# A state-space layer whose late adaLN loads get six buffers instead of three ahead, with x parked in DRAM meanwhile, and a weight cast issued ahead of a Silu

## The chip, the cores and the metric

The kernel runs on one core of one Trainium2 chip. The core has one matrix engine (TensorE, written PE; its weight loads are written PEld), a vector engine (VectorE, DVE), a scalar engine (ScalarE, ACT), a general engine (GpSimd, POOL) and a synchronisation engine (SyncE, SP) that here mainly issues DMA transfers. The metric is the device time of one execution in microseconds (us); the figure for a kernel is the median over its runs.

## The reference, cut to what matters

The model is a trunk of two layers on 512 tokens of width 1024 in float32. Layer 0 mixes tokens by a gated short convolution, layer 1 by a Mamba-2 state-space layer (SSD) with 8 groups of 4 heads; each is followed by a SwiGLU FFN. Every one of the four sub-layers normalises its input, applies a shift, a scale and a gate that come from the conditioning vector c (adaLN), and adds its result to x:

```
mod = (silu(c) @ ada_w + ada_b).reshape(bsz, DEPTH, 2, 3, D_MODEL)
...
z, xbc, dt_raw = split(h @ w_in, [M_D_INNER, M_D_INNER + M_CONV_DIM])
xbc = silu(causal_depthwise_conv(xbc, conv_w) + conv_b)
...
y = ssd_chunked(xs, dt, a, bm, cm) + d_skip * xs
y = rms_normalize((y * silu(z)).reshape(..., g, M_D_INNER // g)) * norm_g
return y @ w_out
...
gate, up = split(h @ w_in, 2);  return (silu(gate) * up) @ w_out
```

`ada_w` is 1024 x 12288, so the product `silu(c) @ ada_w` reads 48 MB for a single row of output. It is not bound to any place in the program: each block of 1024 columns only has to be done before the sub-layer that uses it.

## The kernel before, in words

**Arithmetic.** Matrix products run on PE in a split form: each float32 weight tile is split into a high part (a cast on ACT, `split_w` L212, L230, or `Units.split` L616) and a low part (a subtraction on DVE, L213, L231, L617), and three matmuls (L285 to L287) take the place of one. A weight tile can be used when ACT and then DVE have passed over it.

**The FFNs.** Part of each FFN's first product is computed in "units" (class `Units`; 12 units in the first FFN, 16 in the second) by a scheme of seven products P1 to P7, of 12 matmuls of 128x128x256 each, in place of eight. Three weight sets are split for each unit: X, Y and Z (and a half one, S). The products accumulate in three banks sA, sB, sC; between them small steps (`c11`, `c12`, `c22`, `c21`) move finished quarters to the output and apply the Silu (for a gate, in even units) or the product with the gate (in odd units). For PE, the order in the loop is P1 of unit u, P7 of u-1, P5 of u, P2 of u, P4 of u-1, P6 of u, P3 of u. `c12(v)`, with v = u-1, ends in a Silu on ACT (L677) where v is even, `split_x(u + 1)` casts X of the next unit (ACT L616) and subtracts (DVE L617), and `c22(v)` (DVE L681) drains bank sA, which P4 of u-1 then takes. The same order is written out again in the second FFN.

**The state-space layer.** The eight groups run one behind the other in a pipeline written out by hand, with a loop over g = 1 to 6 for the middle ones. For each group PE makes the projections of x, B, C and z (`project`, `project_z`), the states (`states`, matmuls `st` L1773), the terms from earlier chunks (`yo` L1812) and within a chunk (`yd` L1823), and sums for the norm (`sums`, `ssg` L1855). DVE makes the convolution (`cu` L1677), the inputs of the states (`step_a`: `xw` L1744, `xdt` L1746), the decay factors (`csb` L1800), the running state (`prev` L1778, L1780), the outputs (`y` L1828, `yg`) and the low halves of the weights (L231). Small tables of cumulated sums (cs, ecs) go to DRAM (`cs_d` L1654, `ecs_d` L1656) and are read back broadcast over partitions.

**The late adaLN work.** Four blocks of 1024 columns of `ada_w` are treated here (`late_sums`). Each is eight loads of 512 KB (`ada_st`, 32 in all), each followed by one DVE instruction (`ada_madd` L123 to L127) that multiplies by a value of silu(c) and adds to `ada_acc`; after eight of them `ada_fold` (L140) and one PE matmul (`ada_fin` L147) finish the block. The buffers of the loads come from the pool `ysp` (five buffers, which `ada_acc` and the norm's squares share); load n+3 is requested right behind the sum that uses load n. A call `late(5)` at the head of each round of the loop gives five steps, and `late(1)` ahead of `step_a` one more while g < 5.

**The residual x** lies in four tiles of 128 x 1024 float32 (`xt`, tags x0 to x3 of pool `hp`). The state-space layer uses it at its start, to normalise it, and at its end, to add to it.

**What sets the order.** PE, ACT and DVE run in the order in which the code issues their work (`manual_schedule`). The queue on SP, which issues nearly all loads in this layer, is ordered by the scheduler, and works strictly in that order: a DMA that waits for a buffer holds up those behind it.

Of the kernel before, what the change touches and what calls it, by code (L numbers as in the profile page):

```python
# [8 lines left out]
F32 = mybir.dt.float32  # L9
# [7 lines left out]
P = 128  # L17
T = 512
D = 1024
KD = D // P  # L20
# [11 lines left out]
MUL, ADD, SUB = ALU.mult, ALU.add, ALU.subtract  # L32
# [6 lines left out]
def trunk_kernel(  # L39
# [7 lines left out]
    dma = nc.sync.dma_start  # L47
# [534 lines left out]
    class Units:  # L582
# [34 lines left out]
            dve.tensor_tensor(dst[:, 1], src, dst[:, 0].bitcast(F32), SUB)  # L617

        def split_x(self, u):
            self.split("X", u, whole(), self.staged[u][0][:, 0:8, :])  # L620

        def split_y(self, u):
            self.split("Y", u, whole(), self.staged[u][1].rearrange("p s k f -> p (s k) f"))
# [117 lines left out]
    def whole():  # L741
        return whl_p.tile([P, 2, 8, P], F32R, tag="whl", name="whl")
# [9 lines left out]
    with ExitStack() as ph:  # L752
# [582 lines left out]
        with tc.manual_schedule(engines={PE_ENGINE, mybir.EngineType.SP, mybir.EngineType.Activation,  # L1335
# [51 lines left out]
            for u in range(UN1):  # L1387
                v = u - 1
                end = u == UN1 - 1
                if not end:  # L1390
                    un.fetch(u + 2)
                else:
                    more_n = load_w([(f_w_in[0], (fu + 1) * P, P), (f_w_in[0], DFF + fu * P, P)], later=splits)
                un.product(u, "P1")
                if u:
                    un.c12(v)
                else:
                    up(3, acc[1])
                un.split_x(u + 1)
                if u:  # L1400
                    un.product(v, "P7")
                un.keep(u, "A", 0, lo_)
                un.product(u, "P5")
                if u:
                    un.c22(v)
                low_parts(1)
                un.product(u, "P2")
                un.keep(u, "C", 1, hi_)
                if u:
                    un.product(v, "P4")  # L1410
# [12 lines left out]
                if end:  # L1423
                    for op in splits[2]:
                        op()
                    more_n += load_w([(f_w_in[0], DFF + (fu + 1) * P, P)], later=splits)
                else:
                    un.split_y(u + 1)
                un.product(u, "P3")
                un.keep(u, "A", 0, hi_)  # L1430
                if not end:
                    un.split_s(u + 1)
            u = UN1 - 1
# [151 lines left out]
    with ExitStack() as ph:  # L1585
# [4 lines left out]

        cs_d = dram.tile([NH, T], F32, name="cs_d")
        ecs_d = dram.tile([NH, T], F32, name="ecs_d")

        dt_tok = consts.tile([P, NH, NCH], F32, name="dt_tok")
        cs_tok = consts.tile([P, NH, NCH], F32, name="cs_tok")
# [3 lines left out]
        def flat(ap):  # L1599
            return ap.rearrange("p a b -> p (a b)")  # L1600
# [270 lines left out]
        def late_sums():  # L1871

            uh = tmp.tile([P, 256], F32, tag="uh", name="four", bufs=2)
            sets, st = (64, 72, 80, 88), []

            def load(n):
                if n < KD * len(sets):
                    q0, k = sets[n // KD], n % KD
                    st.append(flat(ysp.tile([P, 2, T], F32, tag="ys", name="ada_st")))
                    dma(st[n], ada_w[k * P:(k + 1) * P, q0 * P:q0 * P + D])  # L1880

            acc = flat(ysp.tile([P, 2, T], F32, tag="ys", name="ada_acc"))
            for n in range(3):
                load(n)
            yield uh[:, 0:P]
            for i, q0 in enumerate(sets):
                for k in range(KD):
                    ada_madd(acc, st[i * KD + k], k)
                    load(i * KD + k + 3)
                    yield  # L1890
                part = uh[:, P + 32 * (i % 2):P + 32 * (i % 2) + 32]
                ada_fold(acc, part)
                fins_late.append(late_end(q0, part))
                yield
# [8 lines left out]
        def late(n):  # L1903
            for _ in range(n):
                next(steps_late, None)
# [30 lines left out]
        with tc.manual_schedule(engines={PE_ENGINE, mybir.EngineType.Activation, mybir.EngineType.DVE}):  # L1936
            cur, nxt, nn = Group(0), Group(1), Group(2)
            nxt.weights(0)
            convs = [cur.conv(i, lead_ps[1 + i]) for i in range(4)]
            rest(0)  # L1940
            raw = dt_raw(lead_ps[0])
# [79 lines left out]
            for g in range(1, NG - 1):  # L2021
# [3 lines left out]
                conv2 = [nxt.project(i) for i in range(2)]  # L2025
                prev.root()
                late_fin()
                late(5)
                nxt.later[3][0]()
                prev.norm()  # L2030
                next(conv2[0])
# [4 lines left out]
                nxt.later[4][0]()  # L2036
                next(conv2[1])
                cur.e_sub(1)
                if g < 5:
                    late(1)  # L2040
                cur.step_a()
                for q in range(2):
                    cur.e_exp(q)
# [34 lines left out]
                cur.sums()  # L2078

            assert next(steps_late, 0) == 0  # L2080
            prev, cur = cur, nxt
            next(parts[0])
            prev.root()
# [53 lines left out]
    with ExitStack() as ph:  # L2137
# [137 lines left out]
        with tc.manual_schedule(engines={PE_ENGINE, mybir.EngineType.SP, mybir.EngineType.Activation,  # L2275
# [60 lines left out]
            for u in range(UN):  # L2336
# [4 lines left out]
                elif last:  # L2341
                    tail = []
                    n12 = load_w([(w1, 21 * P, P), (w1, DFF + 20 * P, P)], later=tail)
                product(u, "P1")
                if u:
                    c12(v)
                else:
                    t_four(1)
                    up(3, acc2)
                split_x(u + 1)  # L2350
                if u:
                    product(v, "P7")
                keep(u, "A", 0, LO)
# [210 lines left out]
```

## Time and profile before

| | |
|---|---|
| Median of 3 runs | 1333.65 us (1332.31 to 1334.56) |
| The profiled execution | 1333.14 us, its span 1331.4 us |
| Mean granted PE clock | 0.997 |
| PE busy | 1310.1 us of the span |
| DVE busy | 1022.0 us |
| ACT busy | 723.0 us |
| POOL busy | 109.8 us |
| First FFN, the units | 253 to 374.5 us from the span's start |
| State-space groups 0 to 6 (between their `ssg` matmuls) | 597.1 to 890.4 us |
| Second FFN, the units | 1035.7 to 1194.1 us |

The profile is of one execution. A row of a group of instructions gives the busy time, the mean length of one in ns, and the idle time ahead of it on its engine with what ended it. A row of waits reads: engine, the tile it was to work on and its line, what it waited for, then total us, number of times, longest. A row of windows gives, for a stretch of time, its length and each engine's busy time with the number of instructions, then the granted PE clock, the mean busy share of the 16 DMA engines and GB/s. A row of the timeline gives the start, the length, the instruction and, in brackets, the idle time ahead of it.

### The profile page before, as it was taken

Reading aid. Unit: us, or ns where it says so; the run is one execution under the profiler, and the core shown is the slowest. Engines: PE = TensorE matmul, PEld = TensorE weight load, DVE = VectorE, ACT = ScalarE, POOL = GpSimd, SP = SyncE. Lnnn points to the kernel's source line nnn. Section 1 sums busy time; section 2 is a strip of 40 time slices with the busy share of each in tenths; the row PEclk is TensorE's granted clock in tenths of the full one; section 3 lists DMA queues with packets and bytes.
Section 4 is the critical chain, followed back from the end, with each engine's and each line's share of the span. In section 5 each row is a group of like instructions: output and inputs, shape, how many; then the busy total and the mean of one; then the engine's idle time right before and its main releaser. Section 6 shows DMA issues by size and latency. Waiting matters only on the chain.

```text
span 1331.4 us, 20439 instructions
## 1 busy us (share of the span) xinstructions
PE 1310.1 (98%) x7869; PEld 1148.7 (86%) x7869; DVE 1022.0 (77%) x1533; ACT 723.0 (54%) x1258; POOL 109.8 (8%) x135
## 2 busy tenths in 40 slices
PE   8999999999999999999999999999999999999998
PEld 7788889999988888898788878888789999998886
DVE  5577767888866887758788978887587777776888
ACT  5333246455432566646765567655574455554665
POOL 0000000111100330000000000000000111101330
PEclk9999999999999999999999999999999999999999
DMA  9767651699878875136654456423251788869871
GB/s 309 231 221 240 222 173 41 175 258 253 206 224 280 204 135 150 45 95 211 206 191 152 140 198 206 127 96 112 95 154 38 197 208 215 210 173 289 183 133 63
DMA packets 224276, 234.85 MB, mean 176 GB/s; under 512 B 10148, under 2 KB 176948, under 8 KB 223156
## 3 DMA queue, kind: packets, MB, share of 16 engines
q1 hardware_dynamic: 203856, 191.03, 46.2%
q0 software_dynamic: 16176, 29.63, 12.8%
q10 hardware_dynamic: 4148, 12.90, 2.9%
q8 instruction: 61, 1.00, 0.3%
q14 instruction: 35, 0.29, 0.1%
HBM read 201.66 MB, written 2.24 MB: 153 GB/s over the span
## 4 chain that ended last, share of the span: by engine, by line
PE 75%; DVE 10%; DMA 9%; ACT 4%; issue 2%; SPq 0%; ACTq 0%; DVEq 0%; POOLq 0%
PE sA L654 10%; PE y L387 8%; PE ip L285 7%; PE ip L287 7%; PE ip L286 7%; PE sC L654 5%; PE cA L2272 4%; DMA ada_st<-in_ada_w_dram 4%; PE cA L1310 3%; PE sB L654 2%; PE li L936 2%; PE li L285 2%; PE li L287 2%; PE li L286 2%; DVE cu L1677 2%; DMA wsu<-wsu 2%
## 5 line engine op out<-in xcount | busy, mean ns | idle before, releaser
L285 PE MATMUL ip<-h,whl 128*128 128x512 f32 x648 | 256.3, 396 | 0.2 <-DVE cv L1036 0.2
L287 PE MATMUL ip<-h,whl 128*128 128x512 f32 x648 | 252.5, 390 | 0.0
L286 PE MATMUL ip<-h,whl 128*128 128x512 f32 x648 | 252.4, 390 | 0.0
L285 PEld LDWEIGHTS ip<-h,whl 128*128 128x128 f32 x648 | 121.9, 188 | 26.5 <-issue 1.8
L287 PEld LDWEIGHTS ip<-h,whl 128*128 128x128 f32 x648 | 121.7, 188 | 25.8
L286 PEld LDWEIGHTS ip<-h,whl 128*128 128x128 f32 x648 | 121.9, 188 | 24.4
L654 PE MATMUL sA<-tq,whl 128*128 128x256 f32 x1008 | 131.3, 284 | 1.7 <-DVE g L681 1.6
L654 PEld LDWEIGHTS sA<-tq,whl 128*128 128x128 f32 x1008 | 125.3, 192 | 3.6 <-DVE g L681 2.9
L127 DVE SCALAR_TENSOR_TENSOR ada_acc<-ada_st,csil,ada_acc 128x1024 f32<-128x1024 f32 x70 | 89.7, 1281 | 28.3 <-DMA ada_st<-in_ada_w_dram 27.4
L231 DVE TENSOR_TENSOR whl<-wst,whl 128x1024 fp32r<-128x1024 f32 x70 | 85.2, 1221 | 25.8 <-ACT whl L230 25.8
L617 DVE TENSOR_TENSOR whl<-wsu,whl 128x1024 fp32r<-128x1024 f32 x58 | 70.9, 1223 | 33.2 <-ACT whl L616 33.2
L387 PE MATMUL y<-whlo,ys 128*128 128x512 f32 x384 | 89.4, 392 | 0.0
L387 PEld LDWEIGHTS y<-whlo,ys 128*128 128x128 f32 x384 | 71.7, 188 | 16.0 <-issue 0.7
L285 PE MATMUL li<-h,whl 128*128 128x256 f32 x288 | 83.2, 289 | 0.0
L287 PE MATMUL li<-h,whl 128*128 128x256 f32 x288 | 81.5, 283 | 0.0
L286 PE MATMUL li<-h,whl 128*128 128x256 f32 x288 | 81.5, 283 | 0.0
L230 ACT CAST whl<-wst 128x1024 fp32r<-128x1024 f32 x70 | 72.8, 1041 | 3.1 <-DMA wst<-in_f_w_in_dram 2.1
L616 ACT CAST whl<-wsu 128x1024 fp32r<-128x1024 f32 x58 | 60.7, 1046 | 14.5 <-PE sB L654 12.2
L1229 POOL DMA_DIRECT2D sg<-sg x28 | 24.4, 871 | 529.5 <-DMA sg<-in_f_w_in_dram 353.0
L1677 DVE SCALAR_TENSOR_TENSOR cu<-ip,cols,cu 128x511 f32<-128x511 f32 (+2 forms) x84 | 62.8, 747 | 3.5 <-ACT cu L1674 1.4
L2272 PE MATMUL cA<-whlo,ao 128*128 128x512 f32 x264 | 61.0, 390 | 0.4 <-DVE c L2477 0.2
L2272 PEld LDWEIGHTS cA<-whlo,ao 128*128 128x128 f32 x264 | 49.3, 188 | 11.5 <-ACT whlo L2237 1.2
(381 smaller groups left out, 2659.5 us busy)
## 6 DMA issues: line engine op xcount, KB each, us to landing
ada_st<-in_ada_w_dram SPq DMA_DIRECT2D x96, 512.0 KB, 6.6
wsu<-in_f_w_in_dram SPq DMA_DIRECT2D x30, 512.0 KB, 5.8
sg<-in_f_w_in_dram SPq DMA_DIRECT2D x56, 256.0 KB, 3.5
wsu<-in_f_w_in_dram SPq DMA_DIRECT2D x56, 256.0 KB, 4.7
wst<-in_m_w_in_dram SPq DMA_DIRECT2D x14, 1024.0 KB, 5.4
wst<-in_f_w_in_dram SPq DMA_DIRECT2D x10, 1024.0 KB, 7.0
wst<-in_m_w_in_dram SPq DMA_DIRECT2D x20, 512.0 KB, 5.2
wst<-in_a_w_in_dram SPq DMA_DIRECT2D x9, 1024.0 KB, 7.0
```

Of the source, the lines that this page charges most:

```text
L127: dve.scalar_tensor_tensor(acc, w, csil[:, k:k + 1], acc, MUL, ADD)
L230: later.append((lambda sw=sw, w=w: act.copy(w[:, 0, :nk, :], sw), lambda sw=sw, w=w: dve.tensor_tensor(w[:, 1, :nk, :], sw, w[:, 0, :nk, : ...
L231: lambda sw=sw, w=w: dve.tensor_tensor(w[:, 1, :nk, :], sw, w[:, 0, :nk, :].bitcast(F32), SUB)))
L285: pe.matmul(dst, w_at(w, 0, kk), a[:, 0, sl], start=start, stop=False)
L286: pe.matmul(dst, w_at(w, 0, kk), a[:, 1, sl], start=False, stop=False)
L287: pe.matmul(dst, w_at(w, 1, kk), a[:, 0, sl], start=False, stop=stop)
L387: pe.matmul(pst, a[:, al, tk], wt[:, wl, kk, :], start=k == 0 and i == 0, stop=k == K - 1 and i == 2, skip_group_check=bool(held))
L616: act.copy(dst[:, 0], src)
L617: dve.tensor_tensor(dst[:, 1], src, dst[:, 0].bitcast(F32), SUB)
L654: pe.matmul(dst, w[:, wl, k0 + k, :], self.moving(q, k, al), skip_group_check=True, start=q in self.FIRST and k == 0 and i == 0, stop=k == ...
L1677: dve.scalar_tensor_tensor(u[:, sft:], pst[:, :T - sft], w[3 - sft], u[:, sft:], MUL, ADD)
L2272: pe.matmul(bank[r][sub], a[:, al, q, tk], w[:, hl, q, :], start=first and k == 0, stop=last and k == 2, skip_group_check=True)
```

## The change: what it does

There are two edits.

First, in the units: `split_x` is taken apart into `high_x` (the ACT cast) and `low_x` (the DVE subtraction), and in both FFNs' loops the cast is issued ahead of `c12(v)`, whose last step can be the Silu. The subtraction stays where it was.

Second, in the state-space layer: x is written to a DRAM tile `x_d` by four DMAs at the layer's start; the late loads with n mod 6 below 4 go to the four buffers of x, the others to pool `ysp`; six loads are requested ahead instead of three; the head of each round takes six steps (five from g = 5), the single step ahead of `step_a` is gone; and behind the loop x is read back into its tiles by four DMAs.

```
+        def high_x(self, u):
+            dst = self.wts["X", u] = whole()
+            act.copy(dst[:, 0], self.staged[u][0][:, 0:8, :])
+        def low_x(self, u):
+            dst = self.wts["X", u]
+            dve.tensor_tensor(dst[:, 1], self.staged[u][0][:, 0:8, :], dst[:, 0].bitcast(F32), SUB)
...
                 un.product(u, "P1")
+                un.high_x(u + 1)
                 if u:
                     un.c12(v)
                 else:
                     up(3, acc[1])
-                un.split_x(u + 1)
+                un.low_x(u + 1)
...
+        x_d = dram.tile([4, P, D], F32, name="x_d")
...
-                    st.append(flat(ysp.tile([P, 2, T], F32, tag="ys", name="ada_st")))
+                    if n % 6 < 4:
+                        st.append(hp.tile([P, D], F32, tag=f"x{n % 6}", name="ada_st"))
+                    else:
+                        st.append(flat(ysp.tile([P, 2, T], F32, tag="ys", name="ada_st")))
...
-            for n in range(3):
+            for n in range(6):
                 load(n)
...
                     ada_madd(acc, st[i * KD + k], k)
-                    load(i * KD + k + 3)
+                    load(i * KD + k + 6)
...
             nxt.weights(0)
+            for t in range(4):
+                dma(x_d[t], xt[t])
...
                 late_fin()
-                late(5)
+                late(6 if g < 5 else 5)
...
                 cur.e_sub(1)
-                if g < 5:
-                    late(1)
                 cur.step_a()
...
             assert next(steps_late, 0) == 0
+            for t in range(4):
+                xt[t] = hp.tile([P, D], F32, tag=f"x{t}", name=f"x{t}")
+                dma(xt[t], x_d[t])
...
                 product(u, "P1")
+                part_of.high_x(u + 1)
                 if u:
                     c12(v)
...
-                split_x(u + 1)
+                part_of.low_x(u + 1)
```

The order of PE's and of POOL's instructions is the same in both kernels. Three places show what moves elsewhere.

On SP, at the start of the state-space layer; `wst` are the layer's weights, `ea` the 128 x 32 table of the decay rates, `ada_st` the late loads. Before:

```order
L221 DMA wst_5583<-in_m_w_in_dram 128x8x256
L1616 DMA ea_5625<-in_m_a_log_dram 128x32
L221 DMA wst_5771<-in_m_w_in_dram 128x8x128 x2
L221 DMA wst_5887<-in_m_w_in_dram 128x8x256
L1654 DMA cs_d_5563<-csb_5751 128x128
L1656 DMA ecs_d_5564<-csb_5751 128x128
L1880 DMA ada_st_5778<-in_ada_w_dram 128x1024
L1880 DMA ada_st_5780<-in_ada_w_dram 128x1024
L1880 DMA ada_st_5782<-in_ada_w_dram 128x1024
```

And after, from the same weight load on:

```order
L221 DMA wst_5584<-in_m_w_in_dram 128x8x256
L1954 DMA x_d_5565<-x0_100 128x1024
L1954 DMA x_d_5565<-x1_101 128x1024
L1894 DMA ada_st_5783<-in_ada_w_dram 128x1024
L1894 DMA ada_st_5785<-in_ada_w_dram 128x1024
L1954 DMA x_d_5565<-x2_102 128x1024
L1954 DMA x_d_5565<-x3_103 128x1024
L1894 DMA ada_st_5787<-in_ada_w_dram 128x1024
L1894 DMA ada_st_5789<-in_ada_w_dram 128x1024
L1627 DMA ea_5630<-in_m_a_log_dram 128x32
L221 DMA wst_5776<-in_m_w_in_dram 128x8x128 x2
L221 DMA wst_5898<-in_m_w_in_dram 128x8x256
```

The four stores and the first four late loads now stand ahead of the table `ea` and of three weight loads; before, all late loads stood behind the stores of cs and ecs.

On DVE, at the head of one round of the loop (g = 4). Before:

```order
L127 SCALAR_TENSOR_TENSOR ada_acc<-ada_st,csil,ada_acc 128x1024 x5
L1869 SCALAR_TENSOR_TENSOR yg_7079<-yg_7079,cols_91,rg 128x512
L1869 SCALAR_TENSOR_TENSOR yg_7096<-yg_7096,cols_91,rg 128x512
L1677 SCALAR_TENSOR_TENSOR cu<-ip,cols_93,cu 128x511
L1677 SCALAR_TENSOR_TENSOR cu<-ip,cols_93,cu 128x510
L1677 SCALAR_TENSOR_TENSOR cu<-ip,cols_93,cu 128x509
L231 TENSOR_TENSOR whl<-wst,whl 128x1024
L127 SCALAR_TENSOR_TENSOR ada_acc<-ada_st,csil,ada_acc 128x1024
L1744 TENSOR_TENSOR xw<-xtok,dte_tok 128x512
L1746 TENSOR_TENSOR xdt<-xtok,dt_tok 128x512
```

And after:

```order
L127 SCALAR_TENSOR_TENSOR ada_acc<-ada_st,csil,ada_acc 128x1024 x6
L1880 SCALAR_TENSOR_TENSOR yg_7090<-yg_7090,cols_91,rg 128x512
L1880 SCALAR_TENSOR_TENSOR yg_7107<-yg_7107,cols_91,rg 128x512
L1688 SCALAR_TENSOR_TENSOR cu<-ip,cols_93,cu 128x511
L1688 SCALAR_TENSOR_TENSOR cu<-ip,cols_93,cu 128x510
L1688 SCALAR_TENSOR_TENSOR cu<-ip,cols_93,cu 128x509
L231 TENSOR_TENSOR whl<-wst,whl 128x1024
L1755 TENSOR_TENSOR xw<-xtok,dte_tok 128x512
L1757 TENSOR_TENSOR xdt<-xtok,dt_tok 128x512
```

The sixth sum has moved from right ahead of `xw` to the head; nothing else moves. It is so in the rounds g = 1 to 4.

On ACT, in an odd unit of the first FFN; L616 is a weight cast, L677 and L683 the Silus, L664 a copy out of a bank. Before:

```order
L616 CAST wss<-wsu 128x512
L677 ACTIVATE g<-g 128x512
L616 CAST whl<-wsu 128x1024
L664 COPY raw_2152<-sA 128x256
L683 ACTIVATE g<-g 128x256
```

And after:

```order
L616 CAST wss<-wsu 128x512
L625 CAST whl<-wsu 128x1024
L686 ACTIVATE g<-g 128x512
L673 COPY raw_2152<-sA 128x256
L692 ACTIVATE g<-g 128x256
```

The cast of X for the next unit and the Silu of the unit before have changed places; DVE's order in the units is unchanged.

More of the change, by code (lines that the diff above doesn't have):

```diff
@@ L619, in split_x @@
         def split_x(self, u):
[L620 removed]
+            self.high_x(u)
+            self.low_x(u)
+        def high_x(self, u):
[4 more added lines that the diff above has]
+            dve.tensor_tensor(dst[:, 1], self.staged[u][0][:, 0:8, :], dst[:, 0].bitcast(F32), SUB)
         def split_y(self, u):
```

## The prediction

> **What bounds the kernel now.** I read the page first (busy shares), then the waits of PE, then the waits of DVE, then windows cut at the group boundaries of the state-space layer and at units of the FFNs, and last the timelines.
>
> ```profile
> span 1331.4 us, 20439 instructions
> PE 1310.1 (98%) x7869; PEld 1148.7 (86%) x7869; DVE 1022.0 (77%) x1533; ACT 723.0 (54%) x1258; POOL 109.8 (8%) x135
> ...
> PE st L1773 <- DVE xdt L1746: 4.0, 2, 2.7
> PE yd L1823 <- DVE y L1828: 1.9, 4, 0.5
> PE yo L1812 <- DVE prev L1780: 1.8, 4, 0.5
> PE sA L654 <- DVE g L681: 1.6, 3, 0.7
> ```
>
> PE is busy 98% of the span, and the change leaves its instructions and their order alone; so only PE's waits can go, 1331.4 - 1310.1 = 21.3 us at most, and time at a lowered clock. The four waits shown are the ones the change can reach: three of the state-space layer (7.7 us), one of the units (1.6 us). All four end with DVE. What DVE waits for in the state-space groups, and how PE's time differs from group to group (0 to 6, a row each):
>
> ```profile
> DVE ada_acc L127 <- DMA ada_st<-in_ada_w_dram: 23.1, 7, 4.9
> ...
> DVE ada_acc L125 <- DMA ada_st<-in_ada_w_dram: 3.0, 1, 3.0
> ...
> 597.10:637.10 40.00, 40.00 (x217) 33.71 (x215) 34.01 (x47) 25.64 (x45) 1.30 (x1) 1.00 0.60 193
> 637.10:682.10 45.00, 42.30 (x217) 34.82 (x216) 38.32 (x49) 29.28 (x48) 1.48 (x1) 0.96 0.54 176
> 682.10:723.70 41.60, 40.68 (x219) 33.98 (x218) 36.53 (x48) 26.43 (x44) 1.47 (x1) 1.00 0.57 178
> 723.70:764.60 40.90, 40.52 (x218) 33.90 (x217) 36.69 (x53) 26.53 (x44) 1.47 (x1) 1.00 0.57 180
> 764.60:808.40 43.80, 41.09 (x218) 33.84 (x217) 36.52 (x48) 26.55 (x44) 1.49 (x1) 1.00 0.56 180
> 808.40:848.80 40.40, 40.40 (x219) 33.97 (x218) 35.19 (x50) 26.36 (x44) 1.48 (x1) 1.00 0.54 169
> 848.80:890.40 41.60, 40.67 (x219) 33.97 (x218) 34.80 (x50) 26.74 (x46) 1.49 (x1) 1.00 0.38 126
> ```
>
> The same work takes PE from 40.0 to 45.0 us. DVE stands 26.1 us at late loads that have not landed. DVE has 34 to 38 us of work in a group of 40, so a wait of 4.9 us, the longest, takes all it has to spare, and it hands over late. Group 4 shows it step by step, DVE first, then PE:
>
> ```profile
> 764.69 3.90 DVE L127 SCALAR_TENSOR_TENSOR ada_acc<-ada_st,csil,ada_acc 128x1024 f32<-128x1024 f32 x3
> 773.51 1.28 DVE L127 SCALAR_TENSOR_TENSOR ada_acc<-ada_st,csil,ada_acc 128x1024 f32<-128x1024 f32 x1 [4.92 <-DMA ada_st<-in_ada_w_dram]
> 776.21 1.29 DVE L127 SCALAR_TENSOR_TENSOR ada_acc<-ada_st,csil,ada_acc 128x1024 f32<-128x1024 f32 x1 [1.42 <-DMA ada_st<-in_ada_w_dram]
> ...
> 783.90 0.68 DVE L1746 TENSOR_TENSOR xdt<-xtok,dt_tok 128x512 f32<-128x512 f32 x1
> ...
> 784.73 1.10 PE L1773 MATMUL st<-xw,btok 128*128 128x256 f32 x4 [1.25 <-DVE xdt L1746]
> 792.65 0.49 PE L1812 MATMUL yo<-ct,prev 128*128 128x128 f32 x2 [0.46 <-DVE prev L1780]
> ```
>
> Three loads had landed, the next two had not: look-ahead three. DVE loses 6.3 us, xdt is done at 784.6, PE, which had then stood for 1.25 us, wanted it at 783.5.
>
> **The change in the state-space layer.** (a) *Look-ahead six.* A group uses six loads, so each load is requested a whole group (40 us) ahead of its sum.
>
> ```profile
> ada_st<-in_ada_w_dram SPq DMA_DIRECT2D x96, 512.0 KB, 6.6
> ```
>
> At 6.6 us in the median, six loads take about 40 us even one behind the other, and they overlap; DMA's share in the groups is 0.38 to 0.60. I cost the loads' waits at zero afterwards. (b) *The moved sum.* 1.28 us of DVE goes from just ahead of `xw` to the head, in the same stretch ahead of `xdt`: nothing won or lost there; the head's `yg` and `cu` come 1.3 us later than they would, but 5 us earlier than now in groups with a wait. In group 4 `xdt` would come 6.3 us earlier, at 778.3, 5 us ahead of PE. The tightest is group 1, where PE stands longest:
>
> ```profile
> 656.40:659.10 2.70, 0.00 (x0) 0.03 (x1) 2.70 (x5) 2.69 (x4) 0.00 (x0) 0.96 0.41 87
> 659.10:662.50 3.40, 3.40 (x9) 2.73 (x10) 3.33 (x6) 0.41 (x2) 0.00 (x0) 0.53 0.68 239
> ...
> 645.88 1.28 DVE L127 SCALAR_TENSOR_TENSOR ada_acc<-ada_st,csil,ada_acc 128x1024 f32<-128x1024 f32 x1 [0.93 <-DMA ada_st<-in_ada_w_dram]
> 650.59 1.28 DVE L127 SCALAR_TENSOR_TENSOR ada_acc<-ada_st,csil,ada_acc 128x1024 f32<-128x1024 f32 x1 [3.43 <-DMA ada_st<-in_ada_w_dram]
> ```
>
> Less 0.93 + 3.43 = 4.4 us, the first xdt, at whose end PE starts at 659.1, is ready at 654.7, and PE wants it at 656.4: 1.7 us to spare. So PE's 2.7 us go, and so do the 3.4 us that follow them at a granted clock of 0.53, which cost 3.4 x 0.47 = 1.6 us. The Trainium skill (TensorE: Matmul & The Clock Gate, "Part 1: The HAM clock gate") has the clock halved after a whole idle window of about 3.4 us; the row here is halved after 2.7 us. Were the dip not tied to this wait, it would stay, and the sum below would come out 1.6 us higher, at 1321.8.
>
> The size of the gain I take from whole groups. In group 5 PE is busy for all its 40.40 us, in group 0 for all its 40.00; the first, which is nearer to the others in its instructions (219 matmuls), is my floor. Groups 1 to 6 together: 45.0 + 41.6 + 40.9 + 43.8 + 40.4 + 41.6 = 253.3, less 6 x 40.4 = 242.4, gives **10.9 us**. Bounds: 13.3 us if every group comes to group 0's 40.0; from below 5.6 us, if only the two waits on xdt (4.0) and the dip (1.6) go.
>
> (c) *The stores and the reload.* SP, and what it waits behind, at the start of the layer:
>
> ```profile
> 530.17 6.20 SPq L221 DMA_DIRECT2D wst<-in_m_w_in_dram  x2
> 575.32 0.34 SPq L1616 DMA_DIRECT2D ea<-in_m_a_log_dram  x1
> ...
> 593.93 0.34 SPq L1654 DMA_DIRECT2D cs_d<-csb  x1
> ...
> 547.72 1.42 DVE L462 SCALAR_TENSOR_TENSOR x<-c,ss,x 128x512 f32<-128x512 f32 x2
> ...
> 559.89 1.41 DVE L462 SCALAR_TENSOR_TENSOR x<-c,ss,x 128x512 f32<-128x512 f32 x2
> ...
> 541.00:575.00 34.00, 33.72 (x239) 31.21 (x238) 25.56 (x63) 24.45 (x65) 0.00 (x0) 1.00 0.01 1
> ```
>
> From 536.4 to 575.3 SP issues nothing and from 541 the DMA engines are idle (share 0.01). The tiles of x are final at 549.1 us (x0 and x1) and 561.3 us (x2 and x3), where the adds shown end. Two stores, two loads, two stores, two loads, 4 MB in all, then fit ahead of 575.3 if a store lands like a load, in 4 to 10 us. No row shows a 512 KB store; from both sides: nothing, up to the slow case below. I take nothing, since the next larger rows, all loads, are that fast. The Trainium skill (DMA: Bandwidth & Descriptors, "Anatomy of one DMA") says that the wait for the write's receipt can be surprisingly long where the target is HBM, with a fit of 2.0 us + bytes/436e3, an estimate of 3.2 us for 512 KB; no run here shows it. The weights of a group that stand behind late loads in the queue meet at most one more 512 KB load ahead of them: 1.6 us, at the 322 GB/s that group 0's row gives for a full share (193 / 0.60). PE waits for no weights in the rows of the groups, so I take nothing; if the cover fails, it is up to 1.6 us in a group. The reload is issued as the last late loads free the buffers, in groups 5 and 6, where DMA's share is 0.54 and 0.38, and is used only when the layer's output is added to x, behind the last group: nothing.
>
> **The change in the units.** Two units of the first FFN take 20.45 us (the row shown, and two more pairs like it up to 328 us), of the second 20.16, which is fourteen products at 1.44 us. The second row is the whole stretch of the first FFN's units; behind the windows stand ACT and DVE in one odd unit:
>
> ```profile
> 267.00:287.45 20.45, 20.42 (x168) 20.22 (x168) 17.11 (x23) 10.56 (x19) 3.45 (x4) 1.00 0.96 250
> 253.00:374.50 121.50, 120.04 (x987) 118.63 (x986) 100.93 (x140) 62.78 (x107) 18.16 (x21) 1.00 0.89 232
> ...
> 1059.30:1079.46 20.16, 20.16 (x171) 20.16 (x170) 14.45 (x20) 10.56 (x18) 3.45 (x4) 1.00 0.85 213
> ...
> 345.12 0.63 ACT L677 ACTIVATE g<-g 128x512 f32<-128x512 f32 x1 [1.52 <-DVE g L672]
> 345.65 1.03 ACT L616 CAST whl<-wsu 128x1024 fp32r<-128x1024 f32 x1
> 346.72 1.23 DVE L617 TENSOR_TENSOR whl<-wsu,whl 128x1024 fp32r<-128x1024 f32 x1 [1.64 <-ACT whl L616]
> 347.86 0.42 DVE L681 SCALAR_TENSOR_TENSOR g<-sA,g 128x256 f32<-128x256 f32 x1
> ```
>
> In an odd unit ACT idles 1.52 us for the Silu's input, runs the Silu, then the cast; DVE's subtraction waits 1.64 us for the cast, and L681, which frees bank sA for P4, queues behind it. With the cast first, it fits in ACT's idle time (1.03 of 1.52), the Silu starts when it does now, and L681 comes up to 1.6 us earlier. PE gains what it waited: 1.6 us in three waits over 0.2 (two in the first FFN, one at the start of the second), and 0.29 us in each of the three pairs at 20.45: **2.5 us**. Bounds: 0, if the cast, put first, only finds X not yet loaded (DMA's share is 0.96 there, but the row shows the cast running right behind the Silu, with no wait for a load); 3.4 us, the excess of the first FFN's 121.5 us over eleven units of 10.08 and one of five products, 7.2 us. In the second FFN there is no more than the one wait, as its pair is at the ideal.
>
> **The sum.** 1333.14 - 10.9 - 2.5 = 1319.7 us for the profiled execution. That execution stands 0.5 us under the median of the three runs, so against the median: **1320.2 us**, 1.0% faster.
>
> **The rivals.**
>
> *Only half of it goes.* The waits on prev and y (3.7 us) could be DVE's own order, its 35 us of work in a group leaving little room. For it: they come four times each, while xdt is late only twice. Against: DVE's order is the same in groups 0 and 5, and PE is busy there for the whole of the group. Then 4.0 + 1.6 + 2.5 = 8.1 us go: 1325.6 us. Chance 0.17.
>
> *Nothing is won.* Late loads stay late since they share the DMA engines with the broadcasts of cs at the head. Against: with six ahead they may take 40 us. Then about 1331 to 1334 us. Chance 0.06.
>
> *Slower: the stores hold up SP.* The only store rows nearby are small and slow:
>
> ```profile
> 593.93 3.80 DMA cs_d<-csb
> ```
>
> That is 64 KB (128 x 128 float32) in 3.8 us. At this rate 512 KB takes 30.4 us; the pair that starts at 549.1 ends at 579.5, loads 0 and 1 wait for it, the second pair ends at 609.9, loads 2 and 3 wait for that, and the table `ea`, issued at 575.3 now, comes 34.6 us later; the decays, and with them PE, wait. 1333.65 + 34.6 - 13.4 = 1354.8 us. Delay begins at 13.1 us a store, and it eats the whole gain at 19.8 us. Against: 3.8 us for 64 KB is more likely fixed cost than rate, as loads of eight times the size take 6.6 us. Chance 0.08.
>
> *More is won.* Groups at 40.0 and units at their ideal: 13.3 + 3.4 = 16.7 us, 1317.0 us. Chance 0.03.
>
> **How the numbers follow.** The forecast has 0.66, its own spread being 1317 to 1324. The measurement of this kernel can tell about 0.2% (2.7 us) from no change: the case of no gain is "same" (0.06), the slow stores, and whatever of the small costs above adds up, "slower" (0.08), the rest "faster" (0.86). The range runs from the fourth rival's 1317.0 to the start of "same", 1331.0; outside lie 0.14 above and about 0.03 below.
>
> **What would show it right or wrong.** In the profile afterwards, the waits of DVE on `ada_st` in the groups gone (26.1 to under 2 us); groups 1 to 6 at 40.0 to 40.6 us each; no window with a clock near 0.5 at 659 us; the waits on xdt, prev and y together under 1 us; pairs of units of the first FFN at 20.16 us; L681 not behind an idle DVE; the stores landing in under 10 us and `ea` issued by 576 us. I am wrong if `ea`, and the cs store behind it, come later, if a first-FFN unit now shows ACT waiting for X ahead of its Silu, or if prev and y hold PE with no load late.

## The result, and the profile after

The changed kernel takes 1321.65 us (median of four runs, 1320.39 to 1322.97) against 1333.97 us before: a ratio of 0.991, with a 95% interval of 0.9893 to 0.9927. That is 12.3 us, or 0.9%, faster, and within 1.5 us of the forecast. The profiled execution is the longest of the four, 1322.97 us; its span is 1320.8 us.

The views that answer to those of before, in the same order: the page's span and busy times of the changed kernel.

```profile
span 1320.8 us, 20455 instructions
PE 1305.8 (99%) x7869; PEld 1148.0 (87%) x7869; DVE 1022.9 (77%) x1533; ACT 724.0 (55%) x1258; POOL 109.7 (8%) x135
```

Windows of its groups 1 to 6 of the state-space layer, a row each, and of the stretch from the first to the last matmul on the units' banks in the first FFN:

```profile
638.90:678.90 40.00, 40.00 (x216) 33.74 (x215) 38.28 (x48) 27.38 (x46) 1.48 (x1) 1.00 0.60 196
678.90:719.20 40.30, 40.30 (x219) 33.99 (x218) 36.19 (x47) 26.25 (x44) 1.48 (x1) 1.00 0.58 183
719.20:759.30 40.10, 40.10 (x218) 33.70 (x216) 36.88 (x52) 26.11 (x44) 1.48 (x1) 1.00 0.59 184
759.30:799.50 40.20, 40.20 (x218) 33.95 (x217) 36.78 (x48) 26.21 (x44) 1.48 (x1) 1.00 0.57 185
799.50:839.80 40.30, 40.30 (x219) 33.96 (x218) 35.73 (x50) 26.25 (x44) 1.48 (x1) 1.00 0.54 170
839.80:880.00 40.20, 40.20 (x218) 33.95 (x217) 34.74 (x50) 26.04 (x45) 1.48 (x1) 1.00 0.45 144
...
253.00:390.30 137.30, 133.60 (x1060) 130.63 (x1059) 110.78 (x150) 67.32 (x112) 18.15 (x21) 1.00 0.88 232
```

The same stretch in the kernel before:

```profile
253.00:388.40 135.40, 133.94 (x1060) 130.61 (x1059) 110.83 (x150) 66.75 (x112) 18.16 (x21) 1.00 0.89 236
```

The state-space half did what it was forecast to do, and a little more: in every group PE is busy the whole time, the six groups take 241.1 us against 253.3, and the granted clock is 1.00 in all of them. DVE waits for no late load, and PE for no xdt, prev or y. The units' half did not: in this execution the stretch in the first FFN is 137.3 us, nearly 2 us longer than before. Its start still went as forecast: a pair of units takes 20.20 us, where it took 20.45, and PE is busy for all of it. The loss comes later, and here are two windows of it behind that pair (before, PE was busy for 19.96 and 20.00 us in the same two windows):

```profile
264.20:284.40 20.20, 20.20 (x171) 20.20 (x170) 17.70 (x24) 11.10 (x20) 3.45 (x4) 1.00 0.99 262
...
325.00:345.00 20.00, 18.19 (x150) 17.79 (x149) 14.29 (x20) 8.90 (x17) 3.46 (x4) 1.00 0.86 214
345.00:365.00 20.00, 18.87 (x158) 18.66 (x157) 15.45 (x26) 8.74 (x15) 1.74 (x2) 1.00 0.75 188
```

PE's waits have other names now, as its waits in this stretch say:

```profile
PE sA L663 <- ACT raw L673: 1.8, 2, 1.1
PE sA L663 <- DVE raw L690: 1.2, 1, 1.2
PE sA L663 <- ACT g L673: 0.7, 1, 0.7
```

And ACT's waits between 325 and 375 us:

```profile
ACT whl L625 <- DMA wsu<-in_f_w_in_dram: 4.5, 4, 2.6
ACT whl L616 <- DMA wsu<-wsu: 3.1, 1, 3.1
```

L625 is the cast of X that was put first: it waits for its load, which is one of the prediction's signs of being wrong, and the copy L673 that frees bank sA for PE queues behind it on ACT. `wsu<-wsu` is a DMA that POOL issues; it adds one weight tile onto another (`add_`, in `Units.fetch`).

The stores, in the grouped DMA issues between 540 and 600 us:

```profile
x_d<-x SPq DMA_DIRECT2D x4, 512.0 KB, 2.6
```

And SP's timeline there:

```profile
547.39 3.94 SPq L1954 DMA_DIRECT2D x_d<-x  x2
562.51 0.99 SPq L1954 DMA_DIRECT2D x_d<-x  x2
565.95 0.99 SPq L1894 DMA_DIRECT2D ada_st<-in_ada_w_dram  x2
577.15 0.33 SPq L1627 DMA_DIRECT2D ea<-in_m_a_log_dram  x1
```

A store of 512 KB lands in 2.6 us, the median of the four, and SP stands free from 567 us on. The table `ea` and the store of cs go out 1.8 us later than before, as everything does there, because the first FFN ended 1.9 us later: with the stores but the units in their old order, in the first of the runs below, they go out at 575.13 and 593.73 us, against 575.32 and 593.93 before.

### The profile page after: what moved, and what is told of

It is laid out like the page before. It is cut to its first block, busy times and chain, and to the rows that moved or that the text cites. A ratio compares the mean times of both kernels' runs of the same rounds, so it can differ in the third digit from the quotient of the medians.

```text
span 1320.8 us, 20455 instructions
## 1 busy us (share of the span) xinstructions
PE 1305.8 (99%) x7869; PEld 1148.0 (87%) x7869; DVE 1022.9 (77%) x1533; ACT 724.0 (55%) x1258; POOL 109.7 (8%) x135
## 4 chain that ended last, share of the span: by engine, by line
PE 90%; DMA 3%; DVE 2%; SPq 2%; ACT 1%; issue 1%; DVEq 0%; ACTq 0%
PE ip L285 11%; PE ip L287 11%; PE ip L286 11%; PE y L387 10%; PE sA L663 10%; PE sC L663 5%; PE cA L2289 4%; PE cA L1319 3%; PE li L285 3%; PE li L287 3%; PE li L286 3%; PE sB L663 3%; DMA wsu<-wsu 2%; PE li L945 1%; PE cD L2289 1%
## 5 line engine op out<-in xcount | busy, mean ns | idle before, releaser
L1238 POOL DMA_DIRECT2D sg<-sg x28 | 24.3, 868 | 533.5 <-DVE whl L213 227.0
L285 PEld LDWEIGHTS li<-h,whl 128*128 128x128 f32 x288 | 55.2, 192 | 0.0
L286 PEld LDWEIGHTS li<-h,whl 128*128 128x128 f32 x288 | 55.2, 192 | 0.0
```

The costliest lines, as they stand in the source:

```text
L285: pe.matmul(dst, w_at(w, 0, kk), a[:, 0, sl], start=start, stop=False)
L286: pe.matmul(dst, w_at(w, 0, kk), a[:, 1, sl], start=False, stop=False)
L1238: pool.dma_start(dst, src, accum_op=ADD)
```

## The experiments

Each kernel is compared with the kernel before on the same chip, whose median was 1333.37, 1333.19 and 1333.08 us in the three sets of four.

### The two halves apart

The state-space half alone: the units are put back (likewise in the second FFN).

```
-                un.high_x(u + 1)
...
-                un.low_x(u + 1)
+                un.split_x(u + 1)
```

> Only the state-space half of the change; the units as before. Theory A (the state-space half is the whole gain, the units' half gives back in the first FFN what it wins there): the profile of the changed kernel has groups 1 to 6 at 241.1 us against 253.3, so 12.2 us less than before, 1321.8 us; the first FFN's units take as long as before. Rival B, the prediction's own sum (10.9 us here, 2.5 us in the units): 1323.1 us. Rival C (the units' half costs the 2.2 us by which the first FFN's units were longer in the profile of the changed kernel, less 0.4 us won in the second FFN): the units undone are a gain, about 1319.9 us.

Measured: 1321.30 us, ratio 0.9912 (0.9899 to 0.9925): 12.1 us faster. The groups take 241.1 us and PE is busy for all of them; theory A and its number hold. By its median this half alone is 0.4 us ahead of the changed kernel, which the runs do not tell apart.

The units' half alone, on the kernel before (likewise in the second FFN):

```
+                un.high_x(u + 1)
...
-                un.split_x(u + 1)
+                un.low_x(u + 1)
```

> Only the units' half: the cast of X ahead of the Silu in both FFNs, the state-space layer as before. The prediction: 2.5 us faster, 1331.5 us. Theory A (the first FFN's units are held by their loads, so what PE wins in the early units it loses in the late ones): within 1 us of before, about 1333.5 us, with new waits of PE after about 330 us in which ACT waits for X's load. Rival C (a net loss): 1335.8 us.

Measured: 1334.74 us, ratio 1.0008 (0.9997 to 1.0019), over twelve runs from 1330.58 to 1338.04, where seventeen of the kernel before lie between 1331.64 and 1335.78. So the 2.5 us are not there in the median; the likeliest value is a loss of about 1 us, between theory A and rival C, and the interval does not tell it from no change. Two of the twelve runs, at 1330.58 and 1330.69 us, do have the forecast's gain; no profile shows what went otherwise in them. The profiled execution is one of the longer ones, 1336.73 us, at 140.2 us for the first FFN's stretch. Its chain between 285 and 345 us, the heading by line and then two rounds of it:

```profile
by line: DMA wsu<-wsu 54.5%; issue 19.3%; ACT whl L616 8.8%; DMA wsu<-in_f_w_in_dram 4.9%; DVE sg L642 4.6%; DVE wsu L646 3.5%; PE sA L663 2.4%; PE sB L663 2.4%; DVE whl L617 0.5%; ACTq L616 0.4%; POOLq L1238 0.1%; SPq L605 0.0%
...
291.70 7.41 DMA wsu<-wsu
...
299.25 1.06 ACT whl L616
...
301.47 0.69 DVE sg L642
302.17 0.54 issue
302.70 5.90 DMA wsu<-wsu
...
314.41 8.07 DMA wsu<-wsu
```

PE holds 5% of this chain; a loop holds most of the rest: the accumulating DMA, the cast of Z that needs its result, the subtraction, two sums on DVE, the next accumulate. The first accumulate ends at 299.11 us, the next starts 3.6 us later, so with an accumulate of 7.4 us a unit takes 11 us, where PE needs 10.08. Behind the second, 2.1 us more pass for which the chain names no wait (`issue`), so that a shorter accumulate, of 5.9 us, gives 11.7 us. In the profile of the state-space half alone the same stretch of the chain is PE's:

```profile
by line: PE sA L663 57.7%; PE sC L663 27.8%; PE sB L663 14.4%; issue 0.2%
```

There 5.7 us of accumulate and 3.6 us behind it fit into a unit, as the grouped DMA issues from 253 to 388 us say (the last figure is the median from issue to landing), first of the state-space half:

```profile
wsu<-wsu POOLq DMA_DIRECT2D x11, 256.0 KB, 5.7
```

And of the units' half:

```profile
wsu<-wsu POOLq DMA_DIRECT2D x11, 256.0 KB, 7.4
```

### The buffers without the moved sum, and the moved sum without the buffers

The state-space half with the sum ahead of `step_a` put back:

```
-                late(6 if g < 5 else 5)
+                late(5)
...
+                if g < 5:
+                    late(1)
                 cur.step_a()
```

> The state-space half without the moved sum: x to DRAM, its four buffers, six loads ahead, but five steps at the head and one ahead of step_a as before. Theory (the buffers and the look-ahead are everything, the place of the sixth sum nothing): as with the move, 12.2 us less than before, 1321.8 us, no wait of DVE for a late load in the groups. Rival (the sum ahead of step_a was itself what made xdt late): some of PE's waits on xdt stay, about 1325 us.

Measured: 1321.98 us, ratio 0.9918 (0.9903 to 0.9932). The six groups in one window:

```profile
637.30:878.50 241.20, 241.20 (x1301) 203.31 (x1300) 218.38 (x290) 158.39 (x267) 8.86 (x6) 1.00 0.55 177
```

They take 241.2 us, and the place of the sixth sum is worth nothing once its load is there.

The opposite, on the kernel before:

```
-                late(5)
+                late(6 if g < 5 else 5)
...
-                if g < 5:
-                    late(1)
```

> The moved sum alone: six steps at the head in g = 1 to 4, but the old buffers and three loads ahead. Theory (DVE's waits for loads are what PE feels): the sixth sum now also waits for its load, which before landed under about 5 us of other DVE work; DVE's waits grow by 1 to 4 us in each of four groups, and the time by 2 to 8 us, 1336 to 1342 us. Rival (sums only at the heads are a gain in themselves): 1330 us or less.

Measured: 1339.26 us, ratio 1.0049 (1.0036 to 1.0062), 5.9 us slower. Waits of DVE in the groups:

```profile
DVE ada_acc L127 <- DMA ada_st<-in_ada_w_dram: 29.8, 11, 5.2
DVE ada_acc L125 <- DMA ada_st<-in_ada_w_dram: 3.6, 1, 3.6
```

And of PE:

```profile
PE st L1773 <- DVE xdt L1746: 8.6, 4, 4.7
PE yo L1812 <- DVE prev L1780: 3.1, 7, 0.5
PE yd L1823 <- DVE y L1828: 2.0, 4, 0.5
```

DVE's waits grow from 26.1 to 33.4 us and PE's from 7.7 to 13.7. With three loads ahead, the sums at the heads alone would have been a loss.

### DVE's delay without a late load

On the state-space half alone, DVE gets six instructions more at the head of each round (`the_acc` holds `ada_acc`, which they multiply by 1):

```
                 late(6 if g < 5 else 5)
+                for _ in range(6):
+                    dve.tensor_scalar(the_acc[0], the_acc[0], 1.0, None, MUL)
```

> The state-space half alone, with six DVE instructions more of 0.75 us each at the head of each round (they multiply ada_acc by 1): 4.5 us of DVE's time in each of six groups, 27 us in all, where the waits for late loads had been 26.1 us. No load is late. Theory (PE's loss before was DVE's lateness and nothing else): xdt, prev and y come late as before; from the room that they have in the profile of the state-space half (xdt 2.8 to 5.7 us, prev 1.6 to 4.1 us ahead of PE) 3.8 us lost in group 1 and 1.2 to 2.0 us in each of the others, 11 us in all: about 1332 us. Rival (the late loads cost through their traffic, DVE's delay itself is covered): 1322 us.

Measured: 1333.27 us, ratio 0.9997 (0.9986 to 1.0008). The whole gain is gone without a single late load. Groups 1 to 6 in one window:

```profile
636.80:890.20 253.40, 246.27 (x1301) 205.17 (x1301) 242.89 (x326) 160.05 (x268) 8.86 (x6) 0.99 0.53 168
```

And PE's waits in the groups:

```profile
PE yo L1822 <- DVE prev L1790: 3.8, 7, 1.3
PE yd L1833 <- DVE y L1838: 2.4, 5, 0.5
PE st L1783 <- DVE xw L1754: 0.9, 1, 0.9
```

253.4 us is the time that the groups took before. So what the late loads cost was DVE's time. How much of it a group can spare before PE feels it comes out alike from both sides, as an estimate: here DVE is busy for 242.9 us against 218.6, 24.3 us more, of which PE loses 12.3, and before it waited 26.1 us, of which PE lost 12.2; that leaves 2.0 and 2.3 us a group.

### How far ahead

The state-space half with four loads ahead, all in x's buffers:

```
-                    if n % 6 < 4:
-                        st.append(hp.tile([P, D], F32, tag=f"x{n % 6}", name="ada_st"))
-                    else:
-                        st.append(flat(ysp.tile([P, 2, T], F32, tag="ys", name="ada_st")))
+                    st.append(hp.tile([P, D], F32, tag=f"x{n % 4}", name="ada_st"))
...
-            for n in range(6):
+            for n in range(4):
...
-                    load(i * KD + k + 6)
+                    load(i * KD + k + 4)
```

> The state-space half alone with four loads ahead instead of six, all in the four buffers of x. Theory (a head takes six sums, so the fifth and sixth loads are requested only behind the head's first and second sum, and take 4 to 10 us at a head): DVE waits 2 to 5 us in most groups, half to all of the gain is lost again, 1326 to 1332 us. Rival (one load more than before is enough): 1321 to 1323 us.

Measured: a median of 1331.24 us, ratio 0.9981 (0.9969 to 0.9993). Four ahead keeps 2 of 12 us; the groups take 250.7 us. DVE's wait in them:

```profile
DVE ada_acc L127 <- DMA ada_st<-in_ada_w_dram: 18.1, 5, 4.9
```

What counts is that a head's six sums find all six loads landed; a fifth that is requested at the head's start comes too late.

### What holds the units

The changed kernel with the sg loads behind the wsu loads on SP:

```
-            if u < self.count:
-                dma(sg[:, 0], self.cols(u, 1, 0))
-                dma(sg[:, 1], self.cols(u, 1, 1))
             if u:
                 dma(st[:, 8:12, :], self.cols(u - 1, 1, 0))
             dma(st[:, 0:8, :], self.cols(u, 0))
             if u:
                 dma(st[:, 12:16, :], self.cols(u - 1, 1, 1))
+            if u < self.count:
+                dma(sg[:, 0], self.cols(u, 1, 0))
+                dma(sg[:, 1], self.cols(u, 1, 1))
```

> The changed kernel, with one edit in the first FFN's and the second FFN's units: a unit's two loads of sg go out behind its three loads of wsu instead of ahead of them. Theory H (with the cast first, DVE frees sg's buffer about 1 us earlier, the sg loads go out earlier and run beside the accumulating DMA wsu<-wsu, which then takes 7 to 8 us instead of 5.5 to 7, and the loop accumulate, load of X, cast, sum, accumulate comes over a unit's 10.08 us): accumulates of 6.5 us or less, units at 10.1 us, the first FFN's units near 118.5 us, and the kernel at about 1319 us. Rival K (the DMA engines are simply full in the first FFN, in whatever order): no better than the state-space half alone, 1321 us or more.

Measured: 1406.86 us, ratio 1.0557 (1.0543 to 1.0572): far from theory H, and "1321 us or more", which rival K has, holds for another reason than K's. The accumulates were short, 4.2 us in the median, but POOL still issues the accumulate of sg ahead of that of wsu, and in this order they start in the trace: the wsu accumulate had to wait for the later sg loads, and a unit took 13.8 us (eleven accumulates start from 255.7 to 393.3 us). In the chain from 290 to 350 us the sg loads hold 38% and the wsu accumulates 31%. So the run does not test what theory H says of the accumulates: the units were slower, and DMA's share in the stretch was 0.72.

The changed kernel with the loads of `ada_w` for the first FFN's units left out behind the third (the sums read these three tiles again and again, so this kernel's adaLN values are others):

```
+                    if len(kept) < 4:
                         st = ada_tile()
                         dma(st.rearrange("p a b -> p (a b)"), ada_w[k * P:(k + 1) * P, c0:c0 + D])
+                        if kept:
+                            kept.append(st)
+                    else:
+                        st = kept[1 + k % 3]
...
+            kept.append(0)
```

> The changed kernel, with the loads of ada_w left out in the first FFN behind its third (the sums read the same three tiles again; so the adaLN values are others, and 5 MB less move in the stretch of the units). Both H and K: with a fifth of the traffic gone there, the accumulates are short, the units take 10.1 us, no wait of PE behind ACT's cast of X; about 1319 us. If the units' late waits stay, the loop is bound by its own latency, and not by traffic from elsewhere: 1321.5 us.

Measured: 1318.28 us, ratio 0.9891 (0.9878 to 0.9905). The first FFN's stretch:

```profile
252.70:385.50 132.80, 132.74 (x1060) 130.44 (x1059) 110.35 (x150) 67.39 (x112) 18.51 (x21) 1.00 0.77 197
```

And the accumulates in it (the last figure is the median from issue to landing):

```profile
wsu<-wsu POOLq DMA_DIRECT2D x11, 256.0 KB, 4.4
```

Here PE is busy all the time: 132.8 us against 135.4 with the old order and 137.3 to 140.2 with the new. So with the cast first and without this traffic no wait of PE is left there; DMA's share is 0.77 here, 0.85 to 0.90 in the others. How much of the 2.6 us against the kernel before is due to the cast, and how much to the missing loads, this run does not say: the old order was not run without them.

The changed kernel with sg behind wsu on both queues, SP (as above) and POOL:

```
+            if u:
+                add_(flat2(st[:, 8:12, :]), flat2(self.staged[u - 1][0][:, 0:4, :]))
             if u < self.count:
                 add_(flat2(sg[:, 0]), flat2(sg[:, 1]))
-            if u:
-                add_(flat2(st[:, 8:12, :]), flat2(self.staged[u - 1][0][:, 0:4, :]))
```

> The changed kernel, with a unit's sg loads behind its wsu loads on SP, and also the sg accumulate behind the wsu accumulate on POOL (in the run before, the short wsu accumulates, 4.2 to 5.9 us, queued on POOL behind the sg ones, which had to wait for the later loads). Theory H: the loop accumulate, load, accumulate is about 3.8 us longer than the accumulate; accumulates under 6.3 us then fit into a unit of 10.08 us, PE waits for no cast of X, the first FFN's units take near 118.5 us: about 1318.7 us. Rival: the sg sums now come too late for Y, and PE waits for these instead: 1325 us or more.

Measured: 1334.40 us, ratio 1.0014 (0.9999 to 1.0030), over twelve runs from 1331.97 to 1341.19. Theory H falls: the accumulates took 6.6 us in the median all the same, and the first FFN's stretch was 141.1 us, the second's units 9 us longer than in the changed kernel. The rival's time came. ACT waited 12.5 us between 300 and 375 us for DVE's sum over sg, but this does not show the rival's mechanism, since the run without the `ada_w` loads has 12.0 us of the same wait between 285 and 375 us and PE busy throughout. For it speaks the chain from 253 to 392 us, in which the loads of sg hold 12% and its accumulates 11%, beside 32% for the accumulates of wsu. The order of these loads is not the remedy.

Four of the first FFN's adaLN sums, and with them their loads, moved behind the units, once with the new order of the units and once with the old:

```
-                if u:
+                if 0 < u < 8:
                     sums(1)
...
-            sums(2)
+            sums(3)
```

(the second edit at four places behind the units).

> The changed kernel, with the adaLN sums of the first FFN's units 8 to 11 moved behind the units (four loads of 512 KB less among the last units). Theory H: the waits of PE behind ACT's cast of X in the last units get shorter, those in units up to 7 stay as they come; 1319.5 to 1321 us, and less spread. Rival (the loop once behind stays behind by its own latency): 1321.5 to 1323 us.

> The same move of the four sums, on the state-space half alone (units in the old order). Control: the units in the old order have 2.9 us of waits that come from ACT's order and one of 0.9 us at the end; the move changes nothing of these, 1321.3 us. If it is slower, the moved sums cost where they now stand.

Measured: 1321.06 us (0.9897 to 0.9923) with the cast first, and 1320.43 us (0.9892 to 0.9918) with the old order; their intervals overlap, and the first lies at the border of its theory and its rival, so it decides nothing between them. In the profiles the stretch is 137.4 us with the cast first (an execution of 1323.07 us, the longest of its four), as long as in the changed kernel, and 134.3 us with the old order, 1.1 us less than in the state-space half alone. The control was expected not to move at all: in this profile, with fewer loads beside the last units, even the old order waits less. That last kernel has the lowest median of all that do the whole of the work, 0.9 us under the state-space half alone, and 1.2 us under the changed kernel, which the runs do not tell apart.

The cast first in the second FFN alone, with the state-space half:

> The state-space half and the cast ahead of the Silu in the second FFN alone. Theory: the one wait of 0.44 us at the start of the second FFN's units goes and nothing else: 1320.9 us, the first FFN as in the state-space half alone. Rival (the cast ahead costs in the second FFN too): 1321.5 us or more.

Measured: 1322.09 us, ratio 0.9919 (0.9906 to 0.9932), profiled at 1324.87 us, the longest of its four. The median is the rival's, though the theory's 1320.9 us lies inside the interval, and the rival's reason does not hold: the second FFN's units take 172.4 us, from the first matmul of their banks to the last, against 172.9 with the old order: 0.5 us is won there. But in this execution the first FFN, in the old order, took 138.7 us, and its chain from 320 us on is led by the accumulate:

```profile
by line: DMA wsu<-wsu 56.7%; issue 12.3%; DMA wsu<-in_f_w_in_dram 11.5%; DVE whl L617 4.8%; ACT whl L616 4.1%; DVE sg L642 3.9%; ACT whl L625 2.0%; DVE whl L629 1.8%; DVE wsu L646 1.4%; DVE raw L698 1.3%; DVE ada_acc L125 0.9%; DVE g L681 0
```

So the old order can fall into the loop too. Of the eight profiles with the old order in the first FFN, this one and the kernel before have accumulates of wsu on their chain; there three of them, of 7.84, 6.77 and 5.66 us, lead it from 341 to 370 us, but the stretch is no longer than in the state-space half alone. Of the three with the cast first and the loads in their order (the changed kernel, the units' half alone, and that with the four sums moved), all have. These three profiles, however, are of the longest execution of four, the third longest of twelve and the longest of four; the shorter executions of these kernels were not profiled.

## Why the prediction was right, and where it was not

**The state-space layer** was right in mechanism and place, and its term too small: 10.9 us were forecast, 12.2 us came (253.3 to 241.1; 12.1 us in the runs of that half alone). The floor of 40.4 us a group, taken from group 5, was 0.2 us too high: 40.0 to 40.3 came. The look-ahead was the cause, as two runs from opposite sides show: the buffers without the move give the whole gain, and DVE's delay without any late load takes it all away again.

**The moved sum** was costed at nothing, which the run without it shows. On its own, without the buffers, it costs 5.9 us; the forecast did not ask for that.

**The dip of the clock** in group 1 went with the wait that led to it, as forecast.

**The stores** landed in 2.6 us, under the forecast's 4 to 10, and `ea` went out 1.8 us later only because all came later; the slower rival never came near its 13.1 us a store. The Trainium skill's fit (DMA: Bandwidth & Descriptors, "Anatomy of one DMA"), an estimate of 3.2 us for that size, is given there for DMAs that GpSimd issues; these stores were issued by SP and took 2.6 us.

**The units** are the step that failed: the sum's term "PE gains what it waited: 2.5 us". The second FFN gave its part (0.5 us). In the first FFN 2.2 us were forecast. The early units went that way (a pair at 20.20 us), but more was lost behind 325 us, and the whole stretch is 1.9 us longer in the profile of the changed kernel. On the chip the half alone is 1 us slower at its likeliest, with runs 7.5 us apart. The forecast named the condition itself, that the cast, put first, finds X not loaded, with DMA's share of 0.96 as the sign; it set this aside because the row of one unit showed no wait for a load. What it did not see is the loop behind X's load: 6.5 us of accumulate (the median before) and 3.6 us of cast, subtraction and sums (as in the run of the half alone) make 10.1 us, which is already a unit's time. The kernel before has three accumulates on its chain, too. So with the old order DVE's wait for the cast and this loop were, by this sum, two causes of nearly the same length; where the loop held, taking the first away left the second, now with the loads' lateness passed on to ACT and PE. Without the `ada_w` loads PE waits no more at all.

That the total came out near the forecast is in part luck: the one term was 1.3 us too small, and the other too large by some 3 us (2.9 by the medians of the changed kernel and of the state-space half alone, 3.9 by the profiles of the changed kernel and the kernel before).

**What stays open** is what tips the units into the loop. The cast first does not by itself go with longer accumulates: their median is 6.5 us in the kernel before and 6.5 in the changed one, 5.4 to 6.7 us over the eight profiles with the old order and 6.0 to 7.4 over the three with the cast first. Less traffic shortens them (4.4 us); moving the sg loads was no remedy; which transfer runs beside them to their harm was not found. That the cast, and not the state of the loads at that moment, tips the loop is not shown: three profiles in three have it with the cast first and two in eight without, but the three are of long executions.

## What to carry to other kernels

A wait for a load costs what it takes from the waiting engine's spare time in that stage, not its length: 26 us of DVE's waits were 12 us of PE's, and 24 us of mere arithmetic were the same 12. Look-ahead should be counted by what a burst consumes: six sums at a head need six loads, and four are little better than three. Before a wait is removed, look for the loop that runs beside it at the same period; here a round of accumulate, cast and sums was the next bound, and it is read by adding up the pieces between one transfer and the next of its kind. And where executions of a kernel lie 7 us apart, one profile shows one of them and not the kernel.

## What the runs showed of the hardware

The half clock does not follow the length of a wait alone. PE stood for 2.70 us in the kernel before and the clock was 0.53 for the next 3.4 us; in the run with the sums moved alone it stood once for 4.68 and once for 2.81 us. PE's timeline and, behind each, the window from about where it starts again:

```profile
660.62 1.62 PE L1773 MATMUL st<-xw,btok 128*128 128x256 f32 x3 [4.68 <-DVE xdt L1746]
661.00:665.00 4.00, 4.00 (x13) 3.14 (x13) 3.93 (x6) 1.01 (x2) 0.00 (x0) 0.65 0.75 248
...
791.96 1.10 PE L1773 MATMUL st<-xw,btok 128*128 128x256 f32 x4 [2.81 <-DVE xdt L1746]
792.00:796.00 4.00, 4.00 (x18) 3.24 (x19) 3.93 (x7) 0.77 (x2) 0.00 (x0) 1.00 0.79 251
```

After 4.68 us the clock is lowered (0.65 over the 4 us), after 2.81 us it is not. The Trainium skill (TensorE: Matmul & The Clock Gate, "Part 1: The HAM clock gate") has a window of 3413 ns that runs freely. The traces agree: in each, the clock is lowered only in whole steps of 3.413 us on one grid, apart from the end of the program (in the run with the sg loads behind on SP alone, the stretches at full clock between two lowered ones are 3, 7 and 14 such steps, 10.24, 23.89 and 47.79 us). Cut on this grid, PE's idle 2.70 us lie with 2.46 us in one window, the 4.68 us fill a whole one, and the 2.81 us fall into two, 0.96 and 1.86 us. Over all fourteen traces the clock was lowered eighteen times, each time behind a window in which PE had been idle for 1.74 us or more, and no window with more than 1.86 us went without. So about half a window was enough here, as an estimate from the traces, in which the ends of matmuls are modelled; a whole idle window was not needed.

And a DMA that adds onto its target, 256 KB, took 4.2 and 4.4 us in the median in the two runs with a DMA share of 0.72 and 0.77 in the first FFN's stretch, and 5.4 to 7.4 us in the others, at 0.84 to 0.91. Within these the two do not go together: the 7.4 us stand at 0.85, and 5.7 us at 0.90.
